# Norm factors spread over the partitions: TensorE transposes of a repeated column in place of fp32 products with the identity

## The chip, the cores and the metric

The kernel runs on one core of one Trainium2 chip. The metric is the device time of one execution in microseconds (us). The core has five engines that run side by side, each its own list of instructions in order: TensorE (PE in the profile; its weight loads are listed apart as PEld), VectorE (DVE), ScalarE (ACT), GpSimd (POOL) and SyncE (SP), which here only issues transfers. An engine waits for another through semaphores. TensorE multiplies a stationary operand, loaded as weights, with a moving one, and writes the result into PSUM, which has eight banks of 128 partitions by 512 fp32 numbers.

## The reference

One layer of a decoder block on 512 tokens with 1024 features, all in fp32: two SwiGLU sublayers with a token-mixing sublayer (gated pooling and dilated attention) between them, each behind an RMSNorm whose scale and shift come from a condition vector, and a last RMSNorm.

```python
def rmsnorm(x, g):
    xf = x.astype(jnp.float32)
    y = xf * lax.rsqrt(jnp.mean(xf * xf, axis=-1, keepdims=True) + EPS)
    return (y * g.astype(jnp.float32)).astype(x.dtype)

def reference(...):
    cond = jax.nn.silu(c)
    h = x
...
        u = modulate(rmsnorm(h, g_norm_ffn1[l]), sh1, sc1)
        h = h + 0.5 * gt1 * swiglu(u, w_ffn1_in[l], w_ffn1_out[l])
        u = modulate(rmsnorm(h, g_norm_mix[l]), sh2, sc2)
        h = h + gt2 * token_mixing(u, cos, sin, w_in[l], ...)
        u = modulate(rmsnorm(h, g_norm_ffn2[l]), sh3, sc3)
        h = h + 0.5 * gt3 * swiglu(u, w_ffn2_in[l], w_ffn2_out[l])
    return rmsnorm(h, g_final)
```

So there are four norms, each with one factor per token: one over the root of the mean square of its features.

## The kernel before

**Layout.** Features lie on the partitions, tokens along the free dimension: the state `H` is eight tiles of 128 features by 512 tokens. A norm factor belongs to a token, so to multiply `H` by it, the row of 512 factors must stand on all 128 partitions.

**Products.** The large products run on TensorE in fp32r. Each weight tile and each activation tile is split into a high and a low part (`whi`, `wlo`; `UH`, `UL` for the normalised input, `HI`, `HK` for the gated one), and three products (high by high, low activation by high weight, high activation by low weight: lines 421 to 423, 751 to 753, 1110 to 1112) give one fp32 product. The high part of a weight is copied by ScalarE (L377), the low part subtracted by VectorE (L389). Many blocks of weights go through seven products in place of eight, whose sums VectorE and GpSimd's accumulating transfers make. SyncE loads the weights in the order in which they are used, some chunks ahead.

**A norm in five steps.** ScalarE squares `H` and VectorE adds the squares into `acc` (128 partitions by 512 tokens). `stats_t` multiplies each 128-token piece of `acc`, as stationary operand, with a tile of ones: the sum over the partitions then stands with tokens on the partitions (L509). ScalarE takes the root into `r4`, one column for 128 tokens (L511), and VectorE the reciprocal (L514). `spread` turns each column round (L519): the column, repeated 128 times by a zero step, is the stationary operand and the identity (`cst` in the profile) the moving one, so that out[m, n] is r4[n] on every partition m. Last, VectorE multiplies `H` by that bank and the scale (`norm_t`, L533), ScalarE adds the shift and rounds to `UH` (L545), and VectorE makes `UL` (L559).

**Where that happens.** In `startup` the first norm covers all 512 tokens: four products at L2101, among warm-up products on tiles that are already there (`warm`, L2035), which keep TensorE busy, and beside VectorE's work on the condition's products (`ada_do`, L448; `ada_fin`, L459). The norms between the sublayers are cut into halves of 256 tokens: `out_tail`, which ends a sublayer, spreads the first half within its last output tile and starts its norm steps; `head`, which begins the next, spreads the second half after eight of its steps. Each is two products. In `head` the products run over the eight 128-feature pieces of `UH` and `UL`, some of which VectorE and ScalarE are still making.

**The end.** `tail_end` does the last norm, again in halves. The first half is spread (L1025) while TensorE still works on the second; ScalarE copies the bank for GpSimd, which does five of the eight multiplications, VectorE three (L956). The second half is spread twice into two banks (L1056, L1057), the first read by VectorE, the second by ScalarE for GpSimd. Stores of 128 KB follow each tile from SyncE's and ScalarE's queues.

**Another transpose.** `at_turn` in the attention turns the probabilities with `nc.tensor.transpose` against the same identity, four pieces of 128 by 128 a call, two in the first block (L1504).

The order of all this is written out by hand. Each engine takes its instructions in program order.

Of the kernel before, what the change touches and what calls it, by code (L numbers as in the profile page):

```python
# [14 lines left out]
P = 128  # L15
# [150 lines left out]
class Kernel:  # L166
# [349 lines left out]
    def spread(self, bank, hs):  # L516

        for t in range(hs.start, hs.stop, P):
            self.nc.tensor.matmul(bank[:, t:t + P], self.r4[:, t // P:t // P + 1].to_broadcast([P, P]), self.ident,  # L519
                                  start=True, stop=True)  # L520
        self.Rn[hs.start] = bank

    def ut(self):
# [1106 lines left out]
    def mix(self):  # L1630
# [14 lines left out]
        with tc.tile_pool(name="rt", bufs=1) as self.rt, tc.tile_pool(name="aw", bufs=2) as self.aw:  # L1645
# [156 lines left out]
            def third():  # L1802
# [8 lines left out]
                                 {1: None, 5: self.bT[0]})  # L1811
            at = [t[:, i * T:(i + 1) * T] for i in range(2) for t in (self.qt[1], self.kt[1])]
            self.banks, self.bi = [used[2], self.bS[0], used[0], used[1]] + spread, 0

        def ends():
            self.at_spread(spread)
            self.at_y(spread, 0)
# [210 lines left out]
    def startup(self):  # L2028
        nc, a = self.nc, self.a
        v, M = nc.vector, nc.tensor.matmul  # L2030


        def warm(n, x):
            for _ in range(n):
                M(self.B[5][:, :P], self.ones, x[:, :P], start=True, stop=True)  # L2035
# [62 lines left out]
        self.ada_do(0)  # L2098

        for n in range(4):  # L2100
            M(self.B[6][:, n * P:(n + 1) * P], self.r4[:, n:n + 1].to_broadcast([P, P]), self.ident, start=True, stop=True)  # L2101
        warm(5, self.H[7])
        self.ada_fin("shift", 0, 1)
        banks = list(self.B)
# [3 lines left out]
        t = self.norm_t(0, 0, full)  # L2108
# [7 lines left out]
        for k in range(KT):  # L2116
            if k + 1 < KT:
# [5 lines left out]
                t = self.norm_t(0, k + 1, full)  # L2123
# [88 lines left out]
```

## Time and profile before

| | |
|---|---|
| median of 3 runs | 968.78 us |
| the three runs | 967.72, 970.51, 968.78 us |
| the profiled execution's own time | 966.33 us |
| its span, from the first to the last instruction | 964.5 us |
| mean granted TensorE clock | 0.998 |
| spread products between and after the sublayers (L519) | 28 records on TensorE |
| spread products at startup (L2101) | 8 records |

The profile is of one execution, and its span is shorter than that execution's time by what lies around it. A row of a group gives the line, the engine, the operation with what it writes and reads, and times; "x28" is a count. In the timeline the first number is the start and the second the length, both in us from the start of the span, and a bracket gives the idle time just ahead and who ended it. In the chain of work that ended last, the second number is how far a piece moved that chain's end. Matmuls are pipelined: one starts before the one ahead has ended, so a record's length is not its price.

### The profile page before, as it was taken

What the parts mean: (1) busy time and instruction counts of PE and PEld (TensorE: products, weight loads), DVE (VectorE), ACT (ScalarE), POOL (GpSimd) and SP (SyncE); (2) the same over time, 40 slices, a digit from 0 to 9 for tenths busy, and PEclk for the clock granted to TensorE, in tenths of its full rate; (3) what the DMA queues carried; (4) which work ended last, traced back from release to release, by engine and by line L of the source; (5) the groups of instructions that cost most, each with busy time, mean ns of one, the idle gap of its engine ahead of it and who ended that gap; (6) DMA issues with size and microseconds to landing.
All of it is one profiled execution on the core that took longest, in us unless ns stands there. A gap on an engine that the chain in (4) does not pass through costs nothing.

```text
span 964.5 us, 18166 instructions
## 1 busy us (share of the span) xinstructions
PE 956.2 (99%) x7296; PEld 898.9 (93%) x7296; DVE 839.8 (87%) x1237; ACT 539.5 (56%) x813; POOL 89.8 (9%) x106
## 2 busy tenths in 40 slices
PE   9999999999999999999999999999999999999997
PEld 7888999999999899788889998998999999999997
DVE  7989999899998779887897777989899888989886
ACT  5443656665755453444565553465665647566655
POOL 0000110101010003006500000000101100110002
PEclk9999999999999999999999999999999999999999
DMA  9857786786767647866366446724757666665632
GB/s 354 284 178 259 195 239 160 198 218 154 211 178 231 196 148 241 259 193 192 79 166 184 121 121 220 240 67 120 184 152 190 165 169 171 163 168 138 170 82 88
DMA packets 54087, 174.71 MB, mean 181 GB/s; under 512 B 7793, under 2 KB 10481, under 8 KB 53746
## 3 DMA queue, kind: packets, MB, share of 16 engines
q1 hardware_dynamic: 44416, 141.29, 44.4%
q0 software_dynamic: 9008, 31.72, 18.2%
q8 instruction: 57, 0.93, 0.4%
q10 hardware_dynamic: 578, 0.53, 0.2%
q14 instruction: 28, 0.23, 0.1%
HBM read 135.36 MB, written 2.24 MB: 143 GB/s over the span
## 4 chain that ended last, share of the span: by engine, by line
PE 97%; issue 1%; DMA 1%; POOL 0%; ACT 0%; DVE 0%; SPq 0%; POOLq 0%
PE bank L753 14%; PE bank L752 14%; PE bank L751 14%; PE bank L421 9%; PE bank L422 9%; PE bank L423 9%; PE bank L1112 5%; PE bank L1111 5%; PE bank L1110 5%; PE bank L2134 2%; PE bank L2136 2%; PE bank L2138 2%; PE bank L1471 1%; PE bank L1780 1%; PE bank L1522 1%; PE bank L1781 1%
## 5 line engine op out<-in xcount | busy, mean ns | idle before, releaser
L389 DVE TENSOR_TENSOR wlo<-raw,whi 128x1024 fp32r<-128x1024 f32 (+3 forms) x150 | 166.3, 1118 | 37.4 <-ACT whi L377 37.2
L751 PE MATMUL bank<-UH,whi 128*128 128x256 f32 x672 | 185.7, 276 | 0.0
L752 PE MATMUL bank<-UL,whi 128*128 128x256 f32 x672 | 185.6, 276 | 0.0
L753 PE MATMUL bank<-UH,wlo 128*128 128x256 f32 x672 | 185.6, 276 | 0.0
L389 DVE TENSOR_TENSOR wlo<-X,whi 128x1024 fp32r<-128x1024 f32 (+3 forms) x133 | 142.2, 1082 | 17.8 <-ACT whi L377 17.6
L377 ACT ACTIVATE whi<-raw 128x1024 fp32r<-128x1024 f32 (+3 forms) x150 | 142.6, 964 | 19.4 <-DMA raw<-wf1o 8.2
L377 ACT ACTIVATE whi<-X 128x1024 fp32r<-128x1024 f32 (+3 forms) x133 | 123.0, 946 | 51.0 <-DVE X L312 46.0
L751 PEld LDWEIGHTS bank<-UH,whi 128*128 128x128 f32 x672 | 126.1, 188 | 0.2
L752 PEld LDWEIGHTS bank<-UL,whi 128*128 128x128 f32 x672 | 126.3, 188 | 0.0
L753 PEld LDWEIGHTS bank<-UH,wlo 128*128 128x128 f32 x672 | 126.1, 188 | 0.0
L751 PE MATMUL bank<-SH,whi 128*128 128x256 f32 x408 | 112.6, 276 | 0.0
L752 PE MATMUL bank<-SL,whi 128*128 128x256 f32 x408 | 112.6, 276 | 0.0
L753 PE MATMUL bank<-SH,wlo 128*128 128x256 f32 x408 | 112.6, 276 | 0.0
L421 PE MATMUL bank<-UH,whi 128*128 128x512 f32 (+1 forms) x272 | 92.8, 341 | 0.0
L422 PE MATMUL bank<-UL,whi 128*128 128x512 f32 (+1 forms) x272 | 91.8, 337 | 0.0
L423 PE MATMUL bank<-UH,wlo 128*128 128x512 f32 (+1 forms) x272 | 91.5, 337 | 0.0
L751 PEld LDWEIGHTS bank<-SH,whi 128*128 128x128 f32 x408 | 76.6, 188 | 0.0
L752 PEld LDWEIGHTS bank<-SL,whi 128*128 128x128 f32 x408 | 76.6, 188 | 0.0
L753 PEld LDWEIGHTS bank<-SH,wlo 128*128 128x128 f32 x408 | 76.6, 188 | 0.0
L1110 PE MATMUL bank<-HI,whi 128*128 128x256 f32 x224 | 61.8, 276 | 0.0
L1111 PE MATMUL bank<-HK,whi 128*128 128x256 f32 x224 | 61.8, 276 | 0.0
L1112 PE MATMUL bank<-HI,wlo 128*128 128x256 f32 x224 | 61.8, 276 | 0.0
(408 smaller groups left out, 2409.4 us busy)
## 6 DMA issues: line engine op xcount, KB each, us to landing
raw<-wmix SPq DMA_DIRECT2D x44, 512.0 KB, 4.4
raw<-wf1i SPq DMA_DIRECT2D x32, 512.0 KB, 5.5
raw<-wf2i SPq DMA_DIRECT2D x30, 512.0 KB, 4.3
ada<-wada SPq DMA_DIRECT2D x23, 512.0 KB, 5.7
X<-raw POOLq DMA_DIRECT2D x23, 512.0 KB, 5.8
xs<-wada SPq DMA_DIRECT2D x17, 512.0 KB, 5.3
X<-wf2i SPq DMA_DIRECT2D x14, 512.0 KB, 4.5
X<-wf1i SPq DMA_DIRECT2D x11, 512.0 KB, 4.4
```

Source lines behind the costliest of these rows:

```text
L377: self.nc.scalar.activation(self.hi[:, y], r[:, x], AF.Copy)
L389: self.nc.vector.tensor_tensor(self.lo[:, y], r[:, x], self.hi[:, y], op=OP.subtract)
L421: M(ps, hi, uh, start=start, stop=False)
L422: M(ps, hi, ul, start=False, stop=False)
L423: M(ps, lo, uh, start=False, stop=stop)
L751: M(o, hi, uh, start=start and p == 0 and k == 0, stop=False, skip_group_check=True)
L752: M(o, hi, ul, start=False, stop=False, skip_group_check=True)
L753: M(o, lo, uh, start=False, stop=k == 3, skip_group_check=True)
L1110: M(o, hi, uh, start=start and m % 2 == 0 and k == 0, stop=False, skip_group_check=True)
L1111: M(o, hi, ul, start=False, stop=False, skip_group_check=True)
L1112: M(o, lo, uh, start=False, stop=k == 1, skip_group_check=True)
L2134: M(b, hi, self.UH[k], start=k == 0, stop=False)
```

## The change

`spread` and the four lines in `startup` use TensorE's transpose mode. The stationary operand is still the repeated column and the moving one still the identity, and the same numbers are written to the same places in the same banks. Eighteen instructions are concerned: fourteen at L519 (two in each of the four half norms between the sublayers, two for the first half of the last norm, four for its second half) and four at L2101. Nothing else is touched, so that every engine has the same instructions in the same order, with the same waits. As a line is gone, lines behind 519 have numbers lower by one in the changed kernel.

```diff
@@ -516,8 +516,7 @@
     def spread(self, bank, hs):
 
         for t in range(hs.start, hs.stop, P):
-            self.nc.tensor.matmul(bank[:, t:t + P], self.r4[:, t // P:t // P + 1].to_broadcast([P, P]), self.ident,
-                                  start=True, stop=True)
+            self.nc.tensor.transpose(bank[:, t:t + P], self.r4[:, t // P:t // P + 1].to_broadcast([P, P]), self.ident)
         self.Rn[hs.start] = bank
 
@@ -2098,7 +2097,7 @@
         self.ada_do(0)
 
         for n in range(4):
-            M(self.B[6][:, n * P:(n + 1) * P], self.r4[:, n:n + 1].to_broadcast([P, P]), self.ident, start=True, stop=True)
+            nc.tensor.transpose(self.B[6][:, n * P:(n + 1) * P], self.r4[:, n:n + 1].to_broadcast([P, P]), self.ident)
         warm(5, self.H[7])
         self.ada_fin("shift", 0, 1)
         banks = list(self.B)
```

## The prediction

> **What bounds the kernel now.** I read the page's busy line first, then the head of the chain that ended last, then TensorE's list of waits.
>
> ```profile
> PE 956.2 (99%) x7296; PEld 898.9 (93%) x7296; DVE 839.8 (87%) x1237; ACT 539.5 (56%) x813; POOL 89.8 (9%) x106
> PE 97%; issue 1%; DMA 1%; POOL 0%; ACT 0%; DVE 0%; SPq 0%; POOLq 0%
> PE bank L2134 <- ACT UH L545: 0.5, 1, 0.5
> ```
>
> TensorE is busy for 99% of the span and carries 97% of the chain. Its longest wait for another engine after the start is 0.5 us, at the first real product. So a TensorE instruction that gets shorter normally moves everything behind it forward, unless an operand is then late. VectorE, 87% busy, is where to look for that.
>
> The changed instructions are few. Their rows, and those of a true transpose that the kernel already has (L1504 turns the attention probabilities against the same identity), are:
>
> ```profile
> L519 PE MATMUL bank<-cst,r x28: 270/274/376, 342.1 to 958.3; 128*128 128x128 f32 x28
> L2101 PE MATMUL bank<-cst,r x8: 274/275/376, 12.5 to 13.4; 128*128 128x128 f32 x8
> L1504 PE MATMUL bank<-cst,prob x60: 270/272/329, 389.8 to 478.6; 128*128 128x128 f32 x60
> ```
>
> The code makes 14 products at L519 and 4 at L2101, and the trace has 28 and 8 records: an fp32 product is **two passes**. L1504 makes 60 transposes (14 calls of four, 2 of two) and has 60 records: an fp32 transpose is **one pass**. The duration of one record is alike (274 and 272 ns), but records overlap, so their spacing is what counts. The chain gives it:
>
> ```profile
> 342.05 0.71 PE bank L519 x4
> 352.46 0.44 PE bank L519 x4
> 627.95 0.44 PE bank L519 x4
> 637.27 0.44 PE bank L519 x4
> 948.49 0.46 PE bank L519 x4
> 389.98 0.44 PE bank L1504 x4
> 403.25 0.88 PE bank L1504 x8
> 404.12 0.23 PE bank L421
> 459.97 1.03 PE bank L1504 x8
> ```
>
> Second column: how far the group moves the end of the chain. Two products (4 records) take 0.44 us, so **0.22 us for a product**. Four transposes take 0.44 and eight 0.88, so **0.11 us for a transpose** and no fixed price for entering or leaving that mode (4 and 8 lie on one line through zero). The late groups (1.03 for 8) give 0.13, the upper end. I take 0.11, as the neighbours of those early groups are products with the weights as stationary operand, as at L519. A pair of products becomes 0.22 us in place of 0.44: 0.22 gained, at least 0.18.
>
> The Trainium skill (TensorE: Matmul & The Clock Gate, Terms) says of transpose mode on trn2 that it is four times faster for FP32. By that a transpose would take 0.22/4 = 0.055 us, and the sum below would be 1.7 us in place of 1.1 (an estimate). The rows say twice, and I go by them.
>
> **The change part by part.** Nothing is moved: on each engine the same instructions stand in the same order with the same waits. Only 18 products become transposes, in seven places.
>
> Startup (L2101, 4 products: 8 passes become 4).
>
> ```profile
> 12.36 1.20 DVE L448 SCALAR_TENSOR_TENSOR ada<-ada,cond 128x1024 f32<-128x1024 f32 x1
> 12.50 1.16 PE L2101 MATMUL bank<-cst,r 128*128 128x128 f32 x8
> 13.50 1.28 PE L2035 MATMUL bank<-H,ones 128*128 128x128 f32 x10
> 13.60 0.16 DVE L459 TENSOR_TENSOR mod<-mod,vecs 128x1 f32<-128x1 f32 x1
> 13.70 0.75 DVE L533 SCALAR_TENSOR_TENSOR ev<-H,mod,bank 128x512 f32<-128x512 f32 x1
> 15.26 2.11 PE L2134 MATMUL bank<-UH,whi 128*128 128x512 f32 x8 [0.48 <-ACT UH L545]
> ```
>
> TensorE would be done 0.45 us earlier, but the reader of the bank, VectorE's L533, stands behind L448 and L459. L459 starts at 13.60, when L448 has just ended, so L533 can gain at most 0.1 us. I take **0**: VectorE hides it. The warm-up products behind (L2035) run 0.45 us earlier, and TensorE's idle time before L2134 grows from 0.48 to about 0.93 us.
>
> The two normalisations between sublayers have two places each. The first pair (342.05, 352.46): behind the first, VectorE makes the head's operands.
>
> ```profile
> 347.71 0.48 DVE L559 SCALAR_TENSOR_TENSOR UL<-ev,mod,UH 128x256 fp32r<-128x256 f32 x1
> 348.51 0.28 PE L422 MATMUL bank<-UL,whi 128*128 128x256 f32 x1
> ```
>
> The third low part of the head is ready at 348.19, and TensorE wants it at 348.51: 0.32 us of slack, more than 0.22. So **0.22** is kept here. At 352.46 the next operands lie microseconds away, and no wait follows: **0.22**.
>
> The third place (627.95) is different.
>
> ```profile
> 627.65 0.48 DVE L582 SCALAR_TENSOR_TENSOR H<-bank,mod,H 128x256 f32<-128x256 f32 x1 [0.25 <-PE bank L423]
> 628.05 1.28 DVE L389 TENSOR_TENSOR wlo<-raw,whi 128x512 fp32r<-128x512 f32 x2
> 629.25 0.87 DVE L533 SCALAR_TENSOR_TENSOR ev<-H,mod,bank 128x256 f32<-128x256 f32 x2
> 630.31 0.48 DVE L559 SCALAR_TENSOR_TENSOR UL<-ev,mod,UH 128x256 fp32r<-128x256 f32 x1 [0.19 <-ACT UH L545]
> 630.93 0.31 PE bank L422
> 632.18 0.39 PE bank L422
> 632.17 0.19 PEld L422 LDWEIGHTS bank<-UL,whi 128*128 128x128 f32 x1 [0.21 <-DVE UL L559]
> ```
>
> Here VectorE is the later one. Its chain starts from a bank that TensorE finished **ahead of** the spread (L582), goes through two weight splits (L389), and starts the norm (L533) at 629.25, when the spread's bank has long been written (628.39). TensorE waits for its results twice: chain pieces of 0.31 and 0.39 where such a product else takes 0.11. A spread that is 0.22 shorter makes these waits 0.22 longer. I take **0**; the other end is 0.22.
>
> The fourth place (637.27) resembles the second: **0.22**. The fifth (948.49, first half of the output) takes 0.46, with the products around it on TensorE, so **0.23**.
>
> The end (957.42, four products, two copies of the factor):
>
> ```profile
> 957.20 0.17 DVE L514 RECIPROCAL r<-r 128x2 f32<-128x2 f32 x1 [1.61 <-ACT r L511]
> 957.42 1.16 PE L519 MATMUL bank<-cst,r 128*128 128x128 f32 x8
> 958.17 2.08 DVE L956 TENSOR_TENSOR out<-out,bank 128x256 f32<-128x256 f32 x6 [0.80 <-PE bank L519]
> 959.08 1.41 POOL L956 TENSOR_TENSOR out<-out,AR 128x256 f32<-128x256 f32 x2 [5.57 <-ACT AR L1058]
> GB/s 0 0 0 0 0 0 0 0 0 33 0 0 0 27 313 186 14 289 236 0 233 350 346 119 0 0 0 0 14 326 346 336 342 342 342 49 0 0 16 0
> ```
>
> (The last row is the transfer rate from 945 to 965 us in slices of 0.5.) VectorE waits for the first copy: a first record of 0.38 us and three more by 0.11 now, one more afterwards. So it starts **0.22** earlier. The second copy, for GpSimd, comes 0.45 earlier. But from 959.0 to 962 the stores run at a flat 340 GB/s, so their end follows from when the first begins, and that hangs on VectorE. I take 0.22; the ends are 0.22 and 0.45.
>
> Sum: 0 + 0.22 + 0.22 + 0 + 0.22 + 0.23 + 0.22 = **1.11 us**. With the lower gain at each place and one more place hidden, 0.7; with nothing hidden, 18 x 0.11 + 0.23 = 2.2. The profiled execution took 966.33 us, its span 964.5, so it would become 965.2. The median of the runs shown, 968.78, lies 2.45 above that execution; the same step there gives **967.7**.
>
> **The rivals.**
>
> (a) *All of it counts*: the wait at 632 and the startup shift too, 1.5 to 2.2 us, 966.6 to 967.3. For it speaks the 97% of TensorE on the chain; against it the two VectorE rows above.
>
> (b) *The change doesn't do what it says*, a transpose with a repeated column taking as long as the product, or the gains being lost in waits that the chain doesn't show: 968.3 to 968.8.
>
> ```profile
> L519 PEld LDWEIGHTS bank<-cst,r x28: 185/189/192, 342.1 to 958.2; 128*128 128x128 f32 x28
> L751 PEld LDWEIGHTS bank<-UH,whi 128*128 128x128 f32 x672 | 126.1, 188 | 0.2
> ```
>
> For it: L1504 transposes real tiles, and a column that is read 128 times over is shown only for products. Against it: loading that column as weights takes 189 ns, a plain tile 188.
>
> (c) *Slower, by the clock at startup*. The place is the idle stretch before L2134.
>
> ```profile
> 1.06 2.50 PE L2035 MATMUL bank<-ones 128*128 128x128 f32 x10 [1.06 <-DVE ones L2040]
> 3.70 2.41 PE L2060 MATMUL bank<-X,ones 128*128 128x512 f32 x4
> 5.95 1.95 PE L2069 MATMUL bank<-ones,AR 128*128 128x128 f32 x16
> ```
>
> Ten records of the warm-up take 2.50 us at the start and 1.28 at 13.50: a cold TensorE is at half speed, and stays so until at most 5.95, 4.9 us after its first product (16 records in 1.95 us are at full pace again). If 0.93 us of idleness made it cold again (0.48 does not, it decides from somewhere above), half of 4.9 us would be lost: 2.5 - 1.1 = 1.4 us slower, 970.2. The Trainium skill (the same page, Part 4: PE-mode transpose) bears on this against the change: transposes don't count as TensorE work for the clock gate. The trace rather speaks against (c): eight transposes (403.25) last 0.88 us, about as long as the new gap, and the product behind them (404.12) takes 0.23, as the cold clock would not allow. The Trainium skill (the same page, Part 1: The HAM clock gate) also asks for an idle window of about 3.4 us before the clock is halved.
>
> **How the numbers follow.** Forecast (0.7 to 1.5 us gained) 0.62; (a) 0.14; (b) 0.16; (c) 0.05; 0.03 for others. Each of these is below 0.3% of the time (2.9 us), about what a measurement of this kernel can tell from no change, so "within 0.3%" gets 0.91. The runs shown spread from 967.72 to 970.51, so a median can stray by 1 us or more: 0.05 for faster, 0.04 for slower. The range goes from (a) less 1.1 us of scatter, 965.5, up to (c), 970.2, which also covers (b) with 1.4 of scatter.
>
> **What would show it right or wrong.** The records at the spread should halve, 36 to 18, with groups of two moving the chain by 0.22. At startup VectorE's L533 should still start about 1.3 us after L448, and the idle time before L2134 should be 0.9, with the 2.11 us of its first eight products unchanged. The wait of TensorE for UL near 632 should grow by about 0.2 in all; if it doesn't, (a). VectorE's last multiplications should start 0.75 us after the reciprocal's start in place of 0.97. Groups of two that still take 0.44, or more records than 18, would make (b). A gain over 2.2 us, or a stall that none of these places has, would make the sum wrong.

## The result, and the profile after

The changed kernel takes 966.15 us (median of 22 runs, 964.78 to 968.30), the kernel before, run beside it, 967.27 (22 runs, 966.34 to 970.68). The ratio is 0.9985, with a 95% interval from 0.9979 to 0.9991: 1.45 us gained, between 0.9 and 2.0. That is a real gain and below 0.3%, "within 0.3%" in the prediction's terms. The forecast step was 1.11 us; the difference of the medians is 1.12. (The prediction's 967.7 hung on the median of the first three runs, 968.78, which the longer series puts at 967.27.)

The changed kernel's span and busy line, and the rows of the spread:

```profile
span 963.7 us, 18130 instructions
PE 954.6 (99%) x7278; PEld 897.1 (93%) x7278; DVE 839.2 (87%) x1237; ACT 539.4 (56%) x813; POOL 88.5 (9%) x106
L519 PE MATMUL bank<-cst,r x14: 270/272/323, 342.8 to 957.4; 128*128 128x128 f32 x14
L2100 PE MATMUL bank<-cst,r x4: 270/272/324, 12.6 to 13.0; 128*128 128x128 f32 x4
L519 PEld LDWEIGHTS bank<-cst,r x14: 132/134/137, 342.8 to 957.3; 128*128 128x128 f32 x14
```

The records have halved, 36 to 18. A record is as long as before (272 ns against 274), and its weight load is shorter (134 ns against 189). The chain that ended last shows what that does:

```profile
342.82 0.43 PE bank L519 x2
353.09 0.22 PE bank L519 x2
637.28 0.22 PE bank L519 x2
948.28 0.23 PE bank L519 x2
```

Where it was 0.44 it is 0.22. At the first place, where TensorE starts from an empty pipeline, 0.71 became 0.43. The third place is missing: the chain leaves TensorE there and goes through VectorE and ScalarE, from the bank that TensorE finished ahead of the spread to the first low part:

```profile
627.82 0.48 DVE H L581
628.30 1.20 DVE wlo L389 x2
629.50 0.40 DVE ev L532
629.93 0.52 ACT UH L544
630.48 0.50 DVE UL L558
631.02 0.38 PE bank L422
632.34 0.24 PE bank L422
```

And at the first place there is a piece that the kernel before doesn't have, the third product with a low part (349.17, 0.24 where its neighbours take 0.11):

```profile
349.05 0.11 PE bank L421
349.17 0.24 PE bank L422
349.40 0.12 PE bank L423
```

At startup and at the end the timeline has:

```profile
12.51 1.20 DVE L448 SCALAR_TENSOR_TENSOR ada<-ada,cond 128x1024 f32<-128x1024 f32 x1
12.64 0.65 PE L2100 MATMUL bank<-cst,r 128*128 128x128 f32 x4
13.83 0.75 DVE L532 SCALAR_TENSOR_TENSOR ev<-H,mod,bank 128x512 f32<-128x512 f32 x1
15.39 2.14 PE L2133 MATMUL bank<-UH,whi 128*128 128x512 f32 x8 [0.98 <-ACT UH L544]
956.76 0.17 DVE L514 RECIPROCAL r<-r 128x2 f32<-128x2 f32 x1 [1.61 <-ACT r L511]
957.45 2.08 DVE L955 TENSOR_TENSOR out<-out,bank 128x256 f32<-128x256 f32 x6 [0.53 <-PE bank L519]
```

VectorE's L532 starts 1.32 us after L448 began, 1.34 before: nothing gained at startup. The last multiplications start 0.69 us after their reciprocal, 0.97 before.

The span fell by 0.8 us only, less than the places add up to. The list of weight-load waits shows where about half a microsecond went: a wait for a weight split at about 305 us, which the first profile of the kernel before doesn't have.

```profile
PEld bank L752 <- DVE wlo L389: 0.5, 1, 0.5
```

Whether this belongs to the change is asked below.

### The profile page after: what moved, and what is told of

It reads as the page before. It is cut to its first block, busy times and chain, and to the rows that moved or that the text cites. A ratio compares the mean times of both kernels' runs of the same rounds, so it can differ in the third digit from the quotient of the medians.

```text
span 963.7 us, 18130 instructions
## 1 busy us (share of the span) xinstructions
PE 954.6 (99%) x7278; PEld 897.1 (93%) x7278; DVE 839.2 (87%) x1237; ACT 539.4 (56%) x813; POOL 88.5 (9%) x106
## 3 DMA queue, kind: packets, MB, share of 16 engines
q0 software_dynamic: 9008, 31.72, 18.2%
## 4 chain that ended last, share of the span: by engine, by line
PE 92%; DVE 3%; DMA 2%; issue 1%; ACT 1%; POOL 0%; SPq 0%; POOLq 0%; DVEq 0%; ACTq 0%
PE bank L752 13%; PE bank L751 13%; PE bank L750 13%; PE bank L421 9%; PE bank L422 9%; PE bank L423 9%; PE bank L1111 4%; PE bank L1110 4%; PE bank L1109 4%; PE bank L2133 2%; PE bank L2135 2%; PE bank L2137 2%; DMA raw<-raw 1%; DVE wlo L389 1%; PE bank L1470 1%
```

## The experiments

### Nine products, nine transposes: the price of one

The spread of ten instructions (both halves of both inner norms, the first half of the last) is written nine times over, once with products and once with transposes.

```diff
-    def spread(self, bank, hs):
+    def spread(self, bank, hs, times=9):
...
+            for _ in range(times):
...
-        self.spread(rB, Bh)
-        self.spread(rC, Bh)
+        self.spread(rB, Bh, 1)
+        self.spread(rC, Bh, 1)
```

> The kernel before, with every spread product made nine times over in the same place of the bank (the two halves of both norms between the sublayers and the first half of the last norm, ten products; startup and the end as they were). 80 products more. If a product costs 0.22 us (two passes of 0.11): 17.6 us more than the kernel before, less at most 0.5 that the waits for VectorE behind the third place can swallow, so 17.1 to 17.6. If products overlap better in a longer row, less than 15.

> The changed kernel, with every spread transpose at the same ten places made nine times over: 80 transposes more. If a transpose costs 0.11 us: 8.8 us over the changed kernel, so with its gain of 1.1 to 1.5 us about 7.4 us over the kernel before, and 9 to 10 us under the nine products. If a transpose of a repeated column costs as much as a product: 16 or more over the kernel before. If it costs a quarter of a product: about 3 over it.

Measured against 967.44 us for the kernel before: 985.64 with products, ratio 1.0187 (1.0170 to 1.0203), 18.2 us more; 974.83 with transposes, ratio 1.0076 (1.0059 to 1.0092), 7.4 us more. The first came 0.6 us above its forecast and the second on it; the two differ by 10.8, where 9 to 10 was expected. The chain at the second place, products first, then transposes:

```profile
357.02 4.02 PE bank L520 x36
```

```profile
354.06 1.97 PE bank L520 x18
```

Eighteen products in 4.02 us, 0.22 each; eighteen transposes in 1.97, 0.11 each. A column that is read 128 times over transposes at the pace of a real tile (0.11 at L1504). Rival (b) is out, and so is a quarter of the product's price.

### VectorE's order ahead of the head

The theory: at the first and the third place the gain is cut by operands that VectorE makes. Two moves give it room: the split of the fourth head chunk (1.2 us) goes behind the norm steps, and the second norm step goes ahead of the last output tile. They are made with transposes and, apart from that, with products.

```diff
-                        step(0)
+                        step(1)
...
-                self.split_lo()
+                if h == 0 or m == ms[0]:
+                    self.split_lo()
...
+        self.split_lo()
+        self.fetch()
         self.stepA = step
```

> The changed kernel, with VectorE's split of the fourth head chunk moved behind the norm steps of the first half, and the second norm step ahead of the last output tile. If VectorE's order made the waits behind the first and third place: they go (0.13 and 0.5 us in the trace of the changed kernel), TensorE's chain has pieces of 0.11 to 0.12 throughout from the spread to the sums of the second half, and the time is 0.6 us under the changed kernel, about 0.2% under the kernel before. If the waits come from the spread's bank itself, they stay, and nothing changes.

> The kernel before, products kept, with the same two moves on VectorE. If VectorE's order is what made TensorE wait at 631 and 632 us: those waits (0.47 us) go, and the time is 0.5 us under the kernel before or not to be told from it. Set beside the transposes with the same moves, the first and third place should then differ by the full 0.28 and 0.22 us; the two kernels should be 1.4 to 1.7 us apart. If the two places can't pay in full for another reason, they differ by the 0.14 and 0.15 of the traces so far.

Neither got faster: 966.96 us with transposes, ratio 0.9995 (0.9987 to 1.0004), and 968.36 with products, 1.0008 (0.9997 to 1.0019); they are 1.4 us apart, as expected, but the gains of 0.6 and 0.5 us that the theory promised are missing. The waits for UL at the two places did go. I take the interval from the start of the spread to the start of the next sums (L509), read from the timelines:

| kernel | first place | third place |
|---|---|---|
| before | 342.05 to 350.44: 8.39 | 627.79 to 635.25: 7.46 |
| changed | 342.82 to 351.07: 8.25 | 627.96 to 635.27: 7.31 |
| two moves, products | 343.24 to 351.62: 8.38 | 630.39 to 637.34: 6.95 |
| two moves, transposes | 342.14 to 350.27: 8.13 | 628.86 to 635.58: 6.72 |

In the old order the transposes gain 0.14 and 0.15; with VectorE out of the way they gain 0.25 and 0.23, the full price to within 0.03. That much of the theory stands. But what the moves won at the third place was taken back at once. The chain of the kernel with both (transposes):

```profile
634.55 1.20 DVE wlo L389 x2
635.75 0.08 DVE mod L1169
635.83 0.38 DVE ev L532
636.22 0.39 DVE UL L558
636.61 0.40 DVE ev L532
637.03 0.51 ACT UH L544
637.54 0.16 ACT r L511
637.72 0.18 DVE r L514
637.95 0.43 PE bank L519 x2
```

The moved split and two more norm steps now stand ahead of the second half's factor, and the spread of the fourth place waits for them: from the sums to that spread it is 2.37 us (635.58 to 637.95) in place of 1.85 (635.27 to 637.12).

### The same at the third place alone, and the changed kernel again

For the next one the first place keeps its order, and the reciprocal of the second half goes ahead of one norm step.

```diff
-                        step(0)
+                        step(1 if nxt == 2 else 0)
...
-                    stepA(min(i, 5) + 2)
+                    stepA(min(i + 2, 4) if n == 2 and i < 4 else min(i, 5) + 2)
```

> The changed kernel once more, for a second profile on another occasion and beside the next kernel. If the wait for a weight split at about 305 us (0.3 us, only in the profile of the changed kernel so far) belongs to the run and not to the change, it may be there or not, and the time is 0.1 to 0.2% under the kernel before. From the spread of each place to the next sums the intervals should be those of the first profile: the first place gives 0.14 net, the third 0.15.

> The changed kernel, with VectorE's order changed at the third and fourth place alone: the split of the fourth head chunk behind the norm steps, the second norm step ahead of the last output tile, and the norm step of the sixth feature piece behind the reciprocal of the second half. If VectorE's order is all that TensorE waits for there: no wait for UL at 631 us, none for the reciprocal at 638, and 0.4 to 0.5 us under the changed kernel run beside it. If VectorE's sum of work between 627 and 640 us is the bound, a wait comes back at another place, and the gain stays under 0.2.

The changed kernel again: 966.65 us against 968.33, ratio 0.9981 (0.9972 to 0.9990). With the third place reordered: 966.25, ratio 0.9977 (0.9968 to 0.9987). The two can't be told apart. The third place is down to 6.72 us, and the wait ahead of the fourth spread is gone too (635.71 to 637.56, 1.85). Now TensorE waits in the head's second half:

```profile
644.96 0.19 PEld L422 LDWEIGHTS bank<-UL,whi 128*128 128x128 f32 x1 [0.28 <-DVE UL L558]
```

From the fourth spread to the last norm's first sums it is 309.15 us (637.56 to 946.71), 308.43 in the changed kernel run beside it (638.12 to 946.55): 0.72 given back for 0.58 won. All of it is lost between 645 and 655 us, but only about 0.37 is this wait. The other 0.35 comes from the products behind it: up to 654.84 they stand 0.118 us apart, in the changed kernel 0.113, with no wait that the profile shows and a granted clock of 1.00 in both. So the second theory of the expectation holds in that a wait came back at another place. That the sum of VectorE's work between 627 and 645 us is the whole bound isn't shown: without the wider spacing the new order would have kept 0.2 us.

### The kernel before again, and transposes at two places

> The kernel before once more, for a second profile of it. If the waits at about 305 us and before the sums at the third place belong to the run, one of them may show here though no spread is changed. The intervals at the spreads should be those of the first profile: 0.71 and 0.44 in the chain.

> Transposes at the first and third place alone (the first halves of the norms between the sublayers), products elsewhere. The first place: 0.28 us gained at the spread and 0.13 to 0.14 given back in a wait for UL before the sums of the second half. The third: 0.22 gained, of which 0.07 is given back. The other places as in the kernel before: 0.44 and 0.46 in the chain, and 0.97 us from the last reciprocal to VectorE's last multiplications. In all about 0.3 us, too little to be told by the time of one run.

For the second of the two, `spread` takes a flag that only `out_tail` sets:

```diff
-    def spread(self, bank, hs):
+    def spread(self, bank, hs, turn=0):
...
+            if turn:
+                self.nc.tensor.transpose(bank[:, t:t + P], ...)
+            else:
...
-                        self.spread(rest[0], A)
+                        self.spread(rest[0], A, 1)
```

The second profile of the kernel before (a run of 968.23 us) gives the same intervals, 8.39 (341.98 to 350.37) and 7.45 (629.70 to 637.15); the changed kernel's second has 8.30 (342.90 to 351.20) and 7.30 (628.97 to 636.27). With transposes at the two places alone the first is 8.25 (344.69 to 352.94), the third 7.41 (631.49 to 638.90): 0.14 and only 0.05, where 0.15 was expected. Up to its second wait for UL the third place does what it does in the changed kernel: from the spread's start to that product it is 4.24 us in both (631.49 to 635.73, and 627.96 to 632.20), 4.39 in the kernel before (627.79 to 632.18). The missing 0.10 lies behind it, where TensorE waits for nothing that the profile shows: the next 24 products take 2.83 us (635.95 to 638.78) in place of 2.73 (632.42 to 635.15), again 0.118 us apart in place of 0.114. All other places stand as in the kernel before. The kernel with transposes at two places took 969.97 us, among runs of the kernel before from 966.55 to 970.33, which tells nothing.

The wait at 305 us is absent from both profiles of the kernel before. But three kernels with its products at startup, which differ from it only later, have it: nine products and the two moves with products, 0.4 and 0.5 us, and the transposes at two places 0.9, with another 0.9 just ahead of it for a result of ScalarE's. Of the seven profiles with transposes at startup six have it, and one (the burst of the next section) hasn't. Up to 305 us the five profiles with products at startup are of the same instructions, so the wait can come and go without the change. That the change makes it more frequent isn't ruled out. It begins at ScalarE's copies of the high parts, in the kernel before and in the changed one:

```profile
297.95 2.10 ACT L377 ACTIVATE whi<-raw 128x1024 fp32r<-128x1024 f32 x3 [1.31 <-DMA raw<-raw]
298.58 2.11 ACT L377 ACTIVATE whi<-raw 128x1024 fp32r<-128x1024 f32 x3 [1.94 <-DMA raw<-raw]
```

They wait 1.3 to 1.4 us for an accumulating transfer in the three profiles without the wait, 1.9 to 2.8 in the nine with it. Why that transfer comes later stays open.

### Two tries on the clock at startup

First the four startup transposes nine times over, so that TensorE does nothing else for 4 us; then the changed kernel without the five warm-up products behind them.

```diff
         for n in range(4):
-            nc.tensor.transpose(self.B[6][:, n * P:(n + 1) * P], ...)
+            for _ in range(9):
+                nc.tensor.transpose(self.B[6][:, n * P:(n + 1) * P], ...)
```

```diff
-        warm(5, self.H[7])
         self.ada_fin("shift", 0, 1)
```

> The changed kernel, with each of the four startup transposes made nine times over: 36 in a row. At 0.11 us each they take 4.0 us, 3.5 more; VectorE's multiplication L532 then waits for them and starts about 3.0 us later (0.5 us were hidden behind VectorE's own work). If transposes count as TensorE work for the clock: the warm-up products behind them keep their 0.11 us a record, and the first 24 real products their 5.8 us. If they don't count: the warm-up products take 0.22 a record, or some of the 24 real products run at half speed, up to 3 us more.

> The changed kernel without the five warm-up products behind the startup transposes, so that TensorE idles from about 13.3 to 15.4 us, 2.1 us in place of 1.0. If the clock outlasts that: the first 24 real products take 5.8 us as before, and the time stays within 0.3 us. If it doesn't: they run at half speed for a time, 1.5 to 3 us more, and the new gap of 1.0 us would have been close to trouble.

One run each: 969.04 and 968.11 us, the kernel before 966.03 beside them. TensorE's timeline with 36 transposes, and the row of the stage that holds nothing else (the last three numbers: granted clock, transfer share, GB/s):

```profile
13.14 4.15 PE L2101 MATMUL bank<-cst,r 128*128 128x128 f32 x36
17.13 1.28 PE L2034 MATMUL bank<-H,ones 128*128 128x128 f32 x10
18.88 2.11 PE L2134 MATMUL bank<-UH,whi 128*128 128x512 f32 x8 [0.48 <-ACT UH L544]
```

```profile
15.00:17.00 2.00, 2.00 (x20) 2.00 (x19) 0.00 (x0) 0.00 (x0) 0.00 (x0) 1.00 1.01 404
```

The warm-up products behind take 1.28 us and the first eight real ones 2.11, as ever: the clock stays at full speed. VectorE's L532 moved from 1.32 to 4.33 us behind L448 (13.00 to 17.33), 3.0 later, so 0.5 was hidden, as expected. The Trainium skill (TensorE: Matmul & The Clock Gate, Part 4: PE-mode transpose) has transposes not count as work for the clock gate. This one run disagrees: 4.15 us of nothing but transposes left the clock at 1.00, while 2.09 us of idling, below, did not.

Without the warm-up products TensorE idled 2.09 us ahead of the first real product:

```profile
15.14 3.67 PE L2132 MATMUL bank<-UH,whi 128*128 128x512 f32 x8 [2.09 <-ACT UH L544]
18.65 1.99 PE L2134 MATMUL bank<-UL,whi 128*128 128x512 f32 x8
```

```profile
15.00:17.00 2.00, 1.85 (x4) 1.50 (x5) 2.00 (x5) 1.20 (x4) 0.00 (x0) 0.54 1.03 412
17.00:19.00 2.00, 2.00 (x7) 1.61 (x6) 1.96 (x5) 1.05 (x1) 0.00 (x0) 0.61 1.02 408
```

The granted clock fell to 0.54, and the first eight products took 3.67 us in place of 2.14. From L532's start to the second group of eight it is 5.06 us (13.59 to 18.65), 3.54 in the changed kernel (13.83 to 17.37): 1.5 us lost. So rival (c) is a real mechanism. The changed kernel's own gap, 0.98 us, was not long enough for it in either of its two profiles; where between 0.98 and 2.09 us it begins, one run each can't tell.

## Why the prediction was right, point by point

What each place gained, from the two pairs of profiles (the first two, and the two taken again):

| place | forecast | first pair | second pair |
|---|---|---|---|
| startup | 0 | 0.02 | 0.00 |
| first | 0.22 | 0.14 | 0.09 |
| second | 0.22 | 0.22 | 0.22 |
| third | 0 | 0.15 | 0.15 |
| fourth | 0.22 | 0.22 | 0.22 |
| fifth | 0.23 | 0.23 | 0.23 |
| end | 0.22 | 0.28 | 0.28 |
| sum | 1.11 | 1.26 | 1.19 |

- **The number.** The gain was forecast at 1.11 us, the medians differ by 1.12, the ratio gives 1.45 (0.9 to 2.0). The time itself, 967.7, was 1.5 too high, because it started from the median of three runs.
- **The price** was right: two passes become one, 0.22 us becomes 0.11, shown at ninefold size.
- **Startup** was right: VectorE's own work hides it, and a burst of transposes long enough to show beyond it showed beyond it less 0.5 us. The idle time ahead of the first product grew to 0.98, forecast 0.93.
- **The first place was too high.** The step that failed is "0.32 us of slack, more than 0.22". The slack was counted to the start of the matmul. TensorE waits at the weight load ahead of it, 0.11 us earlier:

```profile
348.40 0.19 PEld L422 LDWEIGHTS bank<-UL,whi 128*128 128x128 f32 x1
```

In the kernel before, that leaves 0.21 us behind VectorE's 348.19. Part of this is no slack either, as the changed kernel shows, where the same load waits for the same low part:

```profile
348.48 0.48 DVE L558 SCALAR_TENSOR_TENSOR UL<-ev,mod,UH 128x256 fp32r<-128x256 f32 x1
349.02 0.19 PEld L422 LDWEIGHTS bank<-UL,whi 128*128 128x128 f32 x1
```

VectorE is done at 348.96 and the load starts at 349.02, 0.06 later. So 0.15 us was slack. And the gain at the spread was 0.28, not 0.22, since the first record of a transpose that starts from an empty pipeline is shorter too (0.32 against 0.38). With 0.28 against 0.15 a wait of 0.13 had to come, and 0.14 was lost in all (349.17, above). In the second pair 0.19 was lost: about 0.10 in the wait, the rest in the products behind it, which stood 0.118 us apart up to the sums.
- **The third place was too low.** The step that failed is that VectorE's chain "starts from a bank that TensorE finished ahead of the spread", as if all of it did. Its later part starts again from a bank that TensorE finishes behind the spread: in the kernel before, L582 for the last output tile starts at 630.85, just after the last product into that bank (630.54 and 0.28). In the changed kernel that bank is ready at 630.76 (630.48 and 0.28), and L581 follows the norm step ahead of it without a gap (before, then after):

```profile
630.54 0.28 PE L423 MATMUL bank<-v,wlo 128*128 128x256 f32 x1
630.85 0.48 DVE L582 SCALAR_TENSOR_TENSOR H<-bank,mod,H 128x256 f32<-128x256 f32 x1
```

```profile
630.48 0.28 PE L423 MATMUL bank<-v,wlo 128*128 128x256 f32 x1
630.48 0.48 DVE L558 SCALAR_TENSOR_TENSOR UL<-ev,mod,UH 128x256 fp32r<-128x256 f32 x1 [0.19 <-ACT UH L544]
630.88 0.48 DVE L581 SCALAR_TENSOR_TENSOR H<-bank,mod,H 128x256 f32<-128x256 f32 x1
```

From the first of the two L581s to this one it was 3.20 us (627.65 to 630.85), now 3.06 (627.82 to 630.88). That 0.14 is what the place pays. So the waits for UL grew by 0.07 in all, where 0.22 was forecast: the first by 0.22, while the second shrank. By the prediction's own sign this place went most of the way to rival (a).
- **The end** was a size off: 0.28, as at the first place, because it too starts from an empty pipeline. The second copy gave about 0.1 on top (from the last multiplications' start to the span's end 6.33 us before, 6.25 after; 6.34 and 6.23 in the second pair), so the stores hid most of its head start, as argued.
- **Rival (a)**, everything counts, is out by the traces: startup paid nothing, and the first and third place not in full. The time alone, with 0.9 to 2.0 us, wouldn't part it from the forecast. Its upper end was a slip too: 18 x 0.11 = 2.0 has the second copy in it already, and the 0.23 on top has no row behind it. **Rival (c)** has the mechanism right and the price too high (1.5 us measured where 2.5 was worked out), and it needs a longer gap than 0.98 us.

The two misjudged places nearly cancel (0.08 too much, 0.15 too little), so the sum is better than its terms: in that it was lucky.

## What to carry to other kernels

Where a column or tile only has to be turned, a transpose cost half of an fp32 product with the identity here (0.11 us against 0.22), and nothing showed to enter or leave that mode. But even in a kernel whose TensorE is 99% busy, the gain of a few tenths of a microsecond at a place counts only as far as the next operand's maker is ahead. Count that slack to the weight load that waits, not to the matmul, and follow the maker's chain to its last start from the engine you are speeding up, not to its first. Where a second engine is nearly as late all along a stretch, reordering its work can move the wait along, as two orders showed here.

## What the runs showed of the hardware that was not expected

A gap of 2.09 us on TensorE was enough for the granted clock to fall to 0.54 for some 3 us. Ahead of it stood only 0.65 us of transposes, 2.74 us from their start to the next product. The Trainium skill (TensorE: Matmul & The Clock Gate, Part 1: The HAM clock gate) speaks of an idle window of about 3.4 us. In this one run less was enough, and no run here shows where it begins.

The spacing of 0.11 us is the same for one pass of a product with the identity, a transpose, and one pass of a sum with ones (four L509 records in 0.44 us), each with its own load of 128 columns. The Trainium skill (the same page, Part 2, LDWEIGHTS) gives a load P/1.2 ns for P columns, so an estimated 107 ns for 128. That is near the spacing of 0.109 to 0.112 us (1.97 us for 18 transposes, 4.02 for 36 passes), and it would make the load, not the product, what sets this pace. The load's own records are longer (134 and 189 ns) and overlap the products, and no run here separates the two.

The products with 256 moving columns stood at one of two spacings, 0.113 and 0.118 us, at a granted clock of 1.00. The wider one followed some waits and lasted: over 9 us with the third place reordered (645.3 to 654.8), 3 us with transposes at two places alone, and only four products behind the changed kernel's wait at 349. Behind its wait at 632.20 the spacing was 0.114 at once. Over 80 products the difference is 0.35 us, as much as a wait, and it stands in no list of waits. What chooses the spacing stays open.
